# A hybrid decoder step in fp32 on one core: activations laid out with tokens along the columns from end to end, and the feed-forward of both pairs of blocks behind the fourth mixer

## The chip, the cores and the metric

The kernel runs on one core of a Trainium2 chip. The core's engines work side by side, each through its own list of instructions in order: PE (TensorE, matrix products into PSUM), DVE (VectorE), ACT (ScalarE), POOL (GpSimd) and SP (SyncE, which here only issues DMAs). ACT and POOL issue DMAs too. An instruction that needs a result of another engine waits for its semaphore, and everything behind it on the same engine waits with it. The metric is the device time of one execution in microseconds (us). Lower is better.

## The reference

2048 prompt tokens and 32 sample tokens (8 sequences of 4) of width 1024 go through one layer; everything is fp32.

```python
h = _rmsnorm(x, n1)
z = h @ w_in                       # hq hf hi hg | sq sk sv | ga gb
o_hg = hgrn2(hq, hf, hi)           # a gated recurrence over tokens, 4 heads
y_a = (_rmsnorm(o_hg, hg_norm_w) * silu(hg)) @ w_up_a
y_b = sliding_window_attention(sq, sk, sv) @ w_up_b
m = sigmoid(ga) * y_a + sigmoid(gb) * y_b
x = x + m @ w_o
h2 = _rmsnorm(x, n2)
x = x + square(relu(h2 @ w_ff1)) @ w_ff2      # 1024 -> 4096 -> 1024
y = _rmsnorm(x, normf_w)
```

`_rmsnorm` divides each token's row by the root of the mean of its 1024 squares and multiplies by a weight per column.

## The kernel before, in words

**Products.** Each fp32 product is made of three faster ones. Both operands are split into a high part (an ACT CAST to fp32r) and a low part (a DVE subtraction), and PE adds high x high, high x low and low x high. Every weight tile therefore passes a DMA on SP, a cast on ACT and a subtraction on DVE before PE can use it.

**Blocks and pairs.** The prompt is cut into four blocks of 512 tokens; the last also takes the 32 sample tokens. For each block a mixer runs on PE in this order: the input projections, attention, the recurrence, the gates, and last w_o (tile `wob`). Blocks 0 and 1 are pair 0, blocks 2 and 3 pair 1. The feed-forward runs on a whole pair, by one level of Strassen's scheme: FF1 (tiles `fB`, `fC`, `fD`) and FF2 (tile `f`; seven steps, whose results are added into `yacc`). The last step of FF2 is done in two column halves (`jp` = 0 and 1), each with four weight tiles of its own (`hw2T`, `lw2T`). Pair 1's operands have 528 columns per half and run in two chunks of 264; pair 0's have 512. Part of pair 1's input projection is done by Strassen's scheme too (stage z).

**Order of stages.** Block 0, block 1, FF1 and FF2 of pair 0, z, block 2, block 3, FF1 and FF2 of pair 1. Within a stage the code's order is the order on each engine, except where small generators and lists of pending steps (`late`, `todo`, `hook`) put pieces of one step between the products of another.

**Two layouts.** Products over tokens want the features on the partitions (here called transposed, as in `hT`). But x, the output of w_o and the two layer norms have the tokens on the partitions. A norm there is one ACT Square that sums along the row, two small POOL operations (L198, L200) and a scaling (`norm_pre`); then `norm_post` brings it into the transposed layout by 8 PE transposes of 128x128 for each 128 tokens (L225, tiles `tp_ab` for the first norm and `tp_fb` for the second), and DVE multiplies by the weight. w_o has the tokens as the stationary operand and 512 columns of w_o moving, so block 3 takes five token tiles, one of them with 32 rows. At the end of each FF2, `Fin` transposes `yacc` back (L1321, tile `fy`), adds the residual x (L1323), squares (L205), takes the root on POOL and scales (L1333), and stores. In FF2's last step PE does these transposes between its products. The norms of block 2 and 3 are done inside FF2 of pair 0 (tiles `x_n`), those of block 1 inside block 0's w_o (`x_b`).

## Time and profile before

| | |
|---|---|
| three runs | 2918.18, 2920.36, 2922.05 us; median 2920.36 |
| the profiled execution | 2911.64 us, of which the traced span is 2908.8 us; granted TensorE clock 0.991 on average |
| busy, of the span | PE 97%, DVE 59%, ACT 40%, POOL 16% |
| DMA | 471.78 MB, 162 GB/s on average |

A line of the trace has the start, the duration, the engine, the line of the kernel and the operation with its output and inputs; in brackets at its end stands how long the engine had been idle and what it waited for. Matrix products overlap in the array: a product with 512 moving columns is listed with 0.39 us, though the next one starts after less. So what a product costs PE is read from the distance of two starts, not from its listed duration. `x8` at the end of a row says that eight like instructions stand together in it.

### The profile page before, as it was taken

How to read it: one execution, taken by the hardware profiler on the slowest of the kernel's cores; microseconds unless marked ns; L12 is line 12 of the kernel's file. 1: busy time of each engine (PE TensorE's matmuls, PEld its weight loads, DVE VectorE, ACT ScalarE, POOL GpSimd, SP SyncE). 2: the span in 40 equal slices, each digit the busy share in tenths (PEclk: the TensorE clock that was granted, in tenths of full speed). 3: DMA queues.
4: the chain of work that ended last, by engine and by line, in shares of the span. 5: the costliest groups of instructions: out<-in, count | busy, mean ns of one | idle time of the engine just before them, and what ended most of it. 6: DMA issues, size and time to landing. Idle time of an engine off the chain costs nothing.

```text
span 2908.8 us, 50329 instructions
## 1 busy us (share of the span) xinstructions
PE 2814.7 (97%) x20207; PEld 2446.7 (84%) x20207; DVE 1705.9 (59%) x2739; ACT 1161.3 (40%) x2191; POOL 451.0 (16%) x791
## 2 busy tenths in 40 slices
PE   7999999999899999999999999999998999999997
PEld 6778887788788878887899867878888999999997
DVE  5684434734787764555765366446657777654455
ACT  3443334423433344543544433333334333344432
POOL 0110111101221110010310101120113333300001
PEclk9999999999999999999999999999999999999999
DMA  7756342145654475665743423423446444485552
GB/s 254 237 161 221 102 151 65 40 123 159 207 178 147 152 263 185 237 205 210 237 131 109 132 81 132 155 75 105 131 148 212 153 147 147 159 286 193 177 184 97
DMA packets 342354, 471.78 MB, mean 162 GB/s; under 512 B 27212, under 2 KB 216680, under 8 KB 342104
## 3 DMA queue, kind: packets, MB, share of 16 engines
q1 hardware_dynamic: 294096, 343.98, 37.2%
q0 software_dynamic: 33376, 105.76, 10.3%
q10 hardware_dynamic: 14648, 18.83, 1.8%
q8 instruction: 158, 2.59, 0.4%
q14 instruction: 76, 0.62, 0.1%
HBM read 345.15 MB, written 124.35 MB: 161 GB/s over the span
## 4 chain that ended last, share of the span: by engine, by line
PE 41%; DMA 3%; DVE 2%; issue 2%; POOL 1%; ACT 1%; SPq 0%; POOLq 0%; DVEq 0%; ACTq 0%
PE f L1349 3%; PE f L1350 3%; PE f L1351 3%; PE fB_f L238 2%; PE fB_f L240 2%; PE fB_f L239 2%; PE fB_z L238 1%; PE fB_z L240 1%; PE fB_z L239 1%; PE fD_f L240 1%; PE fD_f L238 1%; PE fD_f L239 1%; PE wob L191 1%; PE wob L193 1%; PE wob L192 1%
## 5 line engine op out<-in xcount | busy, mean ns | idle before, releaser
L1349 PE MATMUL f<-f2S,hw2T 128*128 128x264 f32 (+1 forms) x576 | 184.1, 320 | 0.0
L1351 PE MATMUL f<-f2S,lw2T 128*128 128x264 f32 (+1 forms) x576 | 183.5, 319 | 0.0
L1350 PE MATMUL f<-f2S,hw2T 128*128 128x264 f32 (+1 forms) x576 | 183.5, 319 | 0.0
L155 DVE TENSOR_TENSOR lw2T<-lw2T,hw2T 128x1024 fp32r<-128x1024 f32 x64 | 78.2, 1224 | 118.0 <-ACT hw2T L154 117.4
L238 PE MATMUL fB_f<-S,w1T_f 128*128 128x264 f32 (+1 forms) x384 | 123.0, 321 | 3.1 <-ACT c_f L300 2.6
L1349 PE MATMUL f<-f2A,h_w2B 128*128 128x264 f32 (+1 forms) x384 | 122.7, 320 | 0.6 <-ACT c_f L1242 0.6
L239 PE MATMUL fB_f<-S,w1T_f 128*128 128x264 f32 (+1 forms) x384 | 122.3, 319 | 0.0
L1350 PE MATMUL f<-f2A,h_w2B 128*128 128x264 f32 (+1 forms) x384 | 122.3, 319 | 0.0
L1351 PE MATMUL f<-f2A,l_w2B 128*128 128x264 f32 (+1 forms) x384 | 122.3, 319 | 0.0
L240 PE MATMUL fB_f<-S,w1T_f 128*128 128x264 f32 (+1 forms) x384 | 122.2, 319 | 0.0
L154 ACT CAST hw2T<-lw2T 128x1024 fp32r<-128x1024 f32 x64 | 67.3, 1051 | 131.8 <-DMA lw2T<-w_T 127.4
L1349 PEld LDWEIGHTS f<-f2S,hw2T 128*128 128x128 f32 x576 | 108.4, 188 | 7.6 <-DVE hw_ab L416 0.3
L1350 PEld LDWEIGHTS f<-f2S,hw2T 128*128 128x128 f32 x576 | 108.4, 188 | 7.3
L1351 PEld LDWEIGHTS f<-f2S,lw2T 128*128 128x128 f32 x576 | 108.0, 188 | 7.6
L155 DVE TENSOR_TENSOR f2S<-f2S 128x1024 fp32r<-128x1024 f32 (+1 forms) x64 | 79.0, 1240 | 56.1 <-ACT f2S L154 55.6
L230 ACT CAST w1T_f<-w1r_f 128x512 fp32r<-128x512 f32 x128 | 77.2, 619 | 69.2 <-PE fB_f L240 28.9
L231 DVE TENSOR_TENSOR l_w2B<-rw2B,h_w2B 128x1024 fp32r<-128x1024 f32 x48 | 58.8, 1224 | 76.8 <-ACT h_w2B L230 59.1
L231 DVE TENSOR_TENSOR w1T_f<-w1r_f,w1T_f 128x512 fp32r<-128x512 f32 x128 | 87.4, 688 | 23.6 <-ACT w1T_f L230 23.4
L1254 POOL DMA_DIRECT2D u_S<-s_f x144 | 77.7, 541 | 114.0 <-DVE s_f L1249 95.9
L1254 POOL DMA_DIRECT2D u_A<-c_f x104 | 56.2, 540 | 235.3 <-DVE c_f L1238 229.7
L154 ACT CAST f2S<-f2S 128x1024 fp32r<-128x1024 f32 (+1 forms) x64 | 67.9, 1064 | 53.5 <-DMA f2S<-u_S 51.1
L300 ACT COPY c_f<-fB_f 128x264 f32<-128x264 f32 (+1 forms) x80 | 36.1, 451 | 126.4 <-PE fB_f L240 117.3
(857 smaller groups left out, 9505.9 us busy)
## 6 DMA issues: line engine op xcount, KB each, us to landing
w1r_f<-w_ff SPq DMA_DIRECT2D x64, 512.0 KB
lw2T<-w_T SPq DMA_DIRECT2D x64, 512.0 KB
rw2B<-w_ff SPq DMA_DIRECT2D x48, 512.0 KB
f2S<-u_S SPq DMA_DIRECT2D x32, 528.0 KB
ws<-w_ff SPq DMA_DIRECT2D x64, 256.0 KB
r_wob<-w_o SPq DMA_DIRECT2D x32, 512.0 KB
f2S<-u_S SPq DMA_DIRECT2D x32, 512.0 KB
u_S<-s_f POOLq DMA_DIRECT2D x96, 132.0 KB, 2.3
```

The lines of the kernel that those rows point to most:

```text
L154: nc.scalar.copy(hi, F(lo))
L155: nc.vector.tensor_tensor(lo, F(lo), F(hi), ALU.subtract)
L230: nc.scalar.copy(dh, src)
L231: nc.vector.tensor_tensor(dl, src, F(dh), ALU.subtract)
L238: nc.tensor.matmul(ps, wh, ah, start=(first and k == 0), stop=False, skip_group_check=not first)
L239: nc.tensor.matmul(ps, wh, al, start=False, stop=False, skip_group_check=not first)
L240: nc.tensor.matmul(ps, wl, ah, start=False, stop=(last and k == 3), skip_group_check=not first)
L300: nc.scalar.copy(x, u.pB)
L1254: nc.gpsimd.dma_start(us[o][u.n // 4][u.n % 4 * P:(u.n % 4 + 1) * P, u.t0:u.t0 + u.ln], y_)
L1349: nc.tensor.matmul(ps, wh, ah, start=first, stop=False, skip_group_check=cont)
L1350: nc.tensor.matmul(ps, wh, al, start=False, stop=False, skip_group_check=cont)
L1351: nc.tensor.matmul(ps, wl, ah, start=False, stop=lastk, skip_group_check=cont)
```

## The change

The host lays x out transposed (`xT`, features by tokens, the sample tokens ahead of block 3), takes the output transposed (`yT`), and sends all norm weights as columns (`c_cols`). Then all of the kernel stays in the transposed layout:

- **Norms.** The sum over features is now a sum over partitions and over 8 row tiles. `Norm.add` squares one row tile on ACT into `na` or `nq` and POOL adds it on. `rstd_row` then multiplies the sum's columns by a column of ones on PE (one product with one moving column for every 128, 88 or 68 tokens; tile `n`), DVE adds the epsilon, POOL takes the root, PE spreads the result over all partitions by a transpose (tile `rb`), ACT copies it to SBUF, and DVE scales the eight row tiles. The 416 transposes of L225 and L1321 are gone; 88 one-column products and 60 transposes `rb` are new.
- **w_o** runs with its own columns as the stationary operand and the tokens moving: 192 products of 512 columns for a block, in block 3 192 of 288 and 192 of 256.
- **Order of stages:** block 0, block 1, z, block 2, block 3, then FF1 and FF2 of pair 0, then FF1 and FF2 of pair 1. The operand sums of the feed-forward are formed from `h2` in DRAM (`ff_sums`), for pair 0 during block 3's w_o, for pair 1 during FF2 of pair 0, and read back by POOL's DMAs.
- **The end of FF2.** `Fin` has one object for each half of the tokens. For each of 8 row tiles it loads x1 (the residual) into a buffer of the ring that also holds weights (`fx`, through `wtile`), adds, squares (`nq`, in the same ring) and sums; then comes `rstd_row`, and 8 scalings with 8 stores.

```diff
-    def norm_post(hsrc, nr, wcol, name, out):
-        for half in range(2):
-            tp = tp_ps(f"tp_{name}_{half}")
-            for kk in range(4):
-                k = half * 4 + kk
-                nc.tensor.transpose(tp[:, kk * P:kk * P + nr], hsrc[0:nr, k * P:(k + 1) * P], ident[0:nr, 0:nr])
...
+    def rstd_row(dst, sqs, n, tmp, name):
+        w = {256: 128, 512: 128, 264: 88, 528: 88, 544: 68}[n]
+        nt = n // w
+        ps = tp_ps(f"n_{name}")[0:w, 0:nt]
+        for i in range(nt):
+            for j, sq in enumerate(sqs):
+                nc.tensor.matmul(ps[:, i:i + 1], sq[:, i * w:(i + 1) * w], ones, start=(j == 0), stop=(j == len(sqs) - 1))
+        rs = tmp("ns", f"rs_{name}")[0:w, 0:nt]
+        nc.vector.tensor_scalar(rs, ps, EPS, None, ALU.add)
+        nc.gpsimd.tensor_tensor(rs, rs, negh[0:w].broadcast_to([w, nt]), ALU.pow)
+        for t0, ln in chunks_of(n):
+            rb = tp_ps(f"rb_{name}_{t0}")[:, 0:ln]
+            for i in range(ln // w):
+                c = t0 // w + i
+                nc.tensor.transpose(rb[:, i * w:(i + 1) * w], rs[:, c:c + 1].broadcast_to([w, P]), ident[0:w, 0:w])
+            nc.scalar.copy(dst[:, t0:t0 + ln], rb)
...
+        def add(u, x):
+            if u.acc is None:
+                u.acc = u.tmp("na", f"na_{u.N}")[:, 0:u.n]
+                nc.scalar.activation(u.acc, x, AF.Square)
+            else:
+                q = u.tmp("nq", f"nq_{u.N}")[:, 0:u.n]
+                nc.scalar.activation(q, x, AF.Square)
+                nc.gpsimd.tensor_tensor(u.acc, u.acc, q, ALU.add)
...
+        n2 = Norm(wk_tmp, T, n2c, f"f{B}")
+        for n in range(0, KD, 2):
+            uo = [unit_rows(w_o, 4 * kh, 4, n * P, 2 * P, f"wo{B}{n}{kh}") for kh in range(2)]
+            for j in range(n, n + 2):
+                js = slice((j - n) * P, (j - n + 1) * P)
+                for (t0, ln) in segs:
+                    ps = (sw_ps, mm_ps)[j % 2](f"wo{B}{j}_{t0}")
+                    gemm_T(ps, ln, [(uo[k // 4][0][:, k % 4, js], uo[k // 4][1][:, k % 4, js]) for k in range(KD)], m_acts, t0)
+                    xo = x1[:, j, t0:t0 + ln]
+                    nc.vector.scalar_tensor_tensor(xo, ps[:, 0:ln], 0.5, xo, ALU.mult, ALU.add)
+                n2.add(x1[:, j])
+                nc.gpsimd.dma_start(x1d[sb][j * P:(j + 1) * P, z0:z0 + T], x1[:, j])
...
+                def add(f, j):
+                    x = wtile(F32, f"fx_{f.N}{j}")[:, 0:f.ln]
+                    c0 = f.o * Th + f.t0
+                    nc.sync.dma_start(x, x1d[sb][j * P:(j + 1) * P, c0:c0 + f.ln])
+                    tt(f.y(j), f.y(j), x, ALU.add)
+                    f.n.add(f.y(j))
...
+                def out(f, j):
+                    f.n.scale(j, f.y(j))
+                    c0 = off[sb] + f.o * Th + f.t0
+                    (nc.sync if last else nc.gpsimd).dma_start(yT[j * P:(j + 1) * P, c0:c0 + f.ln], f.y(j))
...
+            todo = [lambda j=j: f0.add(j) for j in range(KD)] + [f0.end] + [lambda j=j: f0.out(j) for j in range(KD)]
+            todo += [lambda j=j, f=f: f.add(j) for f in f1 for j in range(4, KD)]
...
                         for g in range(KG):
                             for k in range(4):
...
-                            if not last:
-                                if f0 and g == 2 and (jp or j):
-                                    whole(f0.pop(0))
...
+                            for _ in range(2):
+                                if todo:
+                                    todo.pop(0)()
+                        evac(6, 2 * jp + j, f.t0, f.ln, ps)
+                        f.add(2 * jp + j)
```

Three places show how the order on the engines moves. The first is ACT at the boundary of the two column halves in the last step of pair 0's FF2. Before, the casts of the second half's weights (`hw2T_00_1` and on) stand among the squares of the output norm (`jkf`):

```order
L154 CAST hw2T_03_0_11034<-lw2T_03_0_11035 128x1024
L154 CAST f2A_0_11012<-f2A_0_11012 128x1024 x2
L205 ACTIVATE jkf_10989,fs_0_11127<-nj_10987 128x512 x2
L154 CAST hw2T_00_1_11163<-lw2T_00_1_11164 128x1024
L205 ACTIVATE jkf_10989,fs_128_11221<-nj_10987 128x512 x2
L154 CAST hw2T_01_1_11168<-lw2T_01_1_11169 128x1024
L154 CAST hw2T_02_1_11173<-lw2T_02_1_11174 128x1024
L154 CAST hw2T_03_1_11178<-lw2T_03_1_11179 128x1024
```

With the change, two squares of the first token half's sum (`nq`), the copy of its spread root (`na<-rb`) and two squares of the second token half stand right ahead of the first cast:

```order
L230 ACTIVATE nq_y_19288<-y_0_17440 128x512
L230 ACTIVATE nq_y_19294<-y_0_17441 128x512
L216 COPY na_y_19217<-rb_y_0_19324 128x512
L227 ACTIVATE na_y_19301<-y_0_17442 128x512
L230 ACTIVATE nq_y_19384<-y_0_17443 128x512
L147 CAST hw2T_00_1_19387<-lw2T_00_1_19388 128x1024
L147 CAST hw2T_01_1_19392<-lw2T_01_1_19393 128x1024
L147 CAST hw2T_02_1_19397<-lw2T_02_1_19398 128x1024
```

The first cast of the second half moved behind the whole output norm of the first token half.

The second place is DVE at the same boundary (`y_0_17434` to `17441` are the first token half's eight row tiles, `y_0_17443` is the second one of the other token half, `fx` is the residual, `cols` holds the norm weight). Before, no row of DVE there depends on more than 128 tokens at a time. Now:

```order
L209 TENSOR_SCALAR rs_y_19321<-n_y_19316 128x4
L1284 TENSOR_TENSOR y_0_17442<-y_0_17442,fx_y_19298 128x512
L237 SCALAR_TENSOR_TENSOR y_0_17434<-y_0_17434,cols,na_y_19217 128x512
L237 SCALAR_TENSOR_TENSOR y_0_17435<-y_0_17435,cols,na_y_19217 128x512
L237 SCALAR_TENSOR_TENSOR y_0_17436<-y_0_17436,cols,na_y_19217 128x512
L237 SCALAR_TENSOR_TENSOR y_0_17437<-y_0_17437,cols,na_y_19217 128x512
L237 SCALAR_TENSOR_TENSOR y_0_17438<-y_0_17438,cols,na_y_19217 128x512
L237 SCALAR_TENSOR_TENSOR y_0_17439<-y_0_17439,cols,na_y_19217 128x512
L237 SCALAR_TENSOR_TENSOR y_0_17440<-y_0_17440,cols,na_y_19217 128x512
L1284 TENSOR_TENSOR y_0_17443<-y_0_17443,fx_y_19381 128x512
L237 SCALAR_TENSOR_TENSOR y_0_17441<-y_0_17441,cols,na_y_19217 128x512
L148 TENSOR_TENSOR lw2T_00_1_19388<-lw2T_00_1_19388,hw2T_00_1_19387 128x1024
```

Seven scalings of whole row tiles moved ahead of the addition to `y_0_17443`, whose square is the last row of ACT ahead of the cast above.

The third place is SP in the last step of pair 1's FF2, the end of the program. Before, the weights of the second column half (`lw2T_10_1` to `lw2T_13_1`) stand at its start or between stores:

```order
L1305 DMA f2A_1_26977<-u_A_2_1_19863 128x2x528 x2
L1289 DMA lw2T_13_0_27007<-w_T_236 128x4x256
L1289 DMA lw2T_10_1_27332<-w_T_236 128x4x256
L1305 DMA f2A_1_26984<-u_A_3_1_19864 128x2x528 x2
L1289 DMA lw2T_11_1_27337<-w_T_236 128x4x256
L1334 DMA out_y_sample<-nj_26959 16x512 x2
L1334 DMA out_y_prompt<-fx_1_26960 128x512 x6
L1289 DMA lw2T_12_1_27342<-w_T_236 128x4x256
L1334 DMA out_y_prompt<-fx_1_26960 128x512 x2
L1289 DMA lw2T_13_1_27347<-w_T_236 128x4x256
L1334 DMA out_y_sample<-nj_26959 16x512 x2
L1334 DMA out_y_prompt<-fx_1_26961 128x512 x8
```

With the change, a store of the first token half's last row tile and nine loads of the residual stand ahead of them:

```order
L1293 DMA out_yT<-y_1_23862 128x528
L1283 DMA fx_y_26984<-x1d_96 128x264
L1283 DMA fx_y_26990<-x1d_96 128x264
L1283 DMA fx_y_27008<-x1d_96 128x264
L1283 DMA fx_y_27014<-x1d_96 128x264
L1283 DMA fx_y_27031<-x1d_96 128x264
L1283 DMA fx_y_27037<-x1d_96 128x264
L1283 DMA fx_y_27044<-x1d_96 128x264
L1283 DMA fx_y_27063<-x1d_96 128x264
L1283 DMA fx_y_27106<-x1d_96 128x264
L1250 DMA lw2T_10_1_27113<-w_T_218 128x4x256
L1250 DMA lw2T_11_1_27118<-w_T_218 128x4x256
```

The weights of the second half moved behind eight stores (one is shown) and behind the loads `fx` of the second token half; what the first of these loads needs is the scaling of the last row tile that is stored ahead of it.

More of the change, by code (lines that the diff above doesn't have):

```diff
@@ L734, in tile_hybrid_step @@
             while late:
-                norm_post(*late.pop(0))
+                late.pop(0)()
             for h in range(HH):
@@ new lines, in tile_hybrid_step @@
+                            for _ in range(2):
+                                if todo:
+                                    todo.pop(0)()
+                        evac(6, 2 * jp + j, f.t0, f.ln, ps)
+                        f.add(2 * jp + j)
+                    if jp == 1:
+                        while todo:
+                            todo.pop(0)()
+                        f.end()
+                        for j in range(KD):
+                            f.out(j)
+_INS = ["cache_swa_k", "cache_swa_v", "state_hgrn", "w_in", "sinks", "w_up_a", "w_up_b", "w_o", "w_ff1", "w_ff2"]
```

595 lines of the change are left out of this document (236 added, 359 removed).

## The prediction

> **What bounds the kernel now.** I read the page's busy shares and slices first, then PE's rows around the stage boundaries, then the groups of lines for prices.
>
> ```profile
> span 2908.8 us, 50329 instructions
> PE 2814.7 (97%) x20207; PEld 2446.7 (84%) x20207; DVE 1705.9 (59%) x2739; ACT 1161.3 (40%) x2191; POOL 451.0 (16%) x791
> PE   7999999999899999999999999999998999999997
> PEclk9999999999999999999999999999999999999999
> ```
>
> PE is busy in every slice but the first and last, at full clock; the others have slack on average. So a change pays by what it takes off PE, and costs whatever makes PE wait. What a product costs is the distance of two starts. These rows are PE in the last step of FF2 of pair 0, at the boundary of the column halves:
>
> ```profile
> 1364.02 0.39 PE L1349 MATMUL f<-f2A,hw2T 128*128 128x512 f32 x1
> ...
> 1365.16 0.40 PE L1351 MATMUL f<-f2A,lw2T 128*128 128x512 f32 x1
> 1365.39 1.04 PE L1321 MATMUL fy<-ident,yacc 128*128 128x128 f32 x8
> 1366.19 0.48 PE L1349 MATMUL f<-f2A,hw2T 128*128 128x512 f32 x1
> ...
> 1368.52 0.55 PE L1321 MATMUL fy<-ident,yacc 128*128 128x128 f32 x3 [1.16 <-DVE nj L1323]
> 1369.65 0.50 PE L1351 MATMUL f<-f2A,lw2T 128*128 128x512 f32 x1 [0.58 <-DVE lw2T L155]
> ```
>
> Five products of 512 columns from 1364.02 to 1365.16: 0.228 each. Eight transposes from 1365.39 to 1366.19: 0.10 each, though listed at 0.27. And at this boundary PE waited only 1.16 + 0.58 = 1.74 us. Two more distances, from FF2 of pair 1:
>
> ```profile
> 2874.85 0.29 PE L1349 MATMUL f<-f2A,hw2T 128*128 128x272 f32 x1
> ...
> 2875.98 0.29 PE L1349 MATMUL f<-f2A,hw2T 128*128 128x272 f32 x1
> 2892.77 0.28 PE L1351 MATMUL f<-f2A,lw2T 128*128 128x256 f32 x1
> ...
> 2893.13 0.28 PE L1351 MATMUL f<-f2A,lw2T 128*128 128x256 f32 x1
> ```
>
> 272 columns: 1.13 / 9 = 0.126. 256 columns: 0.36 / 3 = 0.12. In proportion 288 cost 0.133.
>
> **The change, part by part.** The sum is made against the profiled execution, 2911.64, and the difference is put on the median of the runs, 2920.36, which lies 8.7 us above it.
>
> (a) The transposes removed: 416.
>
> ```profile
> L225 PE MATMUL tp_fb<-ident,y_b x64: 270/272/328, 407.5 to 1907.1; 128*128 128x128 f32 x64
> L225 PE MATMUL tp_fb<-ident,h_b x64: 270/273/424, 738.3 to 2211.8; 128*128 128x128 f32 x64
> L225 PE MATMUL tp_ab<-ident,x_n x64: 270/272/273, 1138.3 to 1320.8; 128*128 128x128 f32 x64
> L225 PE MATMUL tp_ab<-ident,x_first x32: 271/347/476, 10.6 to 23.9; 128*128 128x128 f32 x32
> L1321 PE MATMUL fy<-ident,yacc x144: 270/272/329, 1361.8 to 2894.7; 128*128 128x128 f32 x128, 128*16 128x128 f32 x16
> ```
>
> The 32 of `x_first` belong to the start (e). 384 x 0.10 = -38. All lie in PE's order, so all count while PE is the bound. The Trainium skill ("TensorE: Matmul & The Clock Gate", Part 4) gives about 275 ns for a transpose in a kernel's context; by that the term would be 384 x 0.275 = -106. The listed 272 agrees with the page, but the distance of starts does not, so the sum doesn't use it.
>
> (b) w_o of block 3: 5 token tiles x 48 = 240 products of 512 columns become 192 of 288 and 192 of 256: 192 x 0.253 - 240 x 0.228 = -6. The other blocks keep 192 of 512. The last step of pair 1's FF2 is cut 264 + 264 instead of 272 + 256: nothing.
>
> (c) New on PE: 56 one-column products and 56 spreading transposes (32 and 4 more at the start). The trace has no one-column product; the nearest row is the transpose, 0.10. As an fp32 product may be two passes, a product costs 0.10 to 0.20: 5.6 to 11, the transposes 5.6. I take +12.
>
> For the waits these prices are needed:
>
> ```profile
> L1073 POOL TENSOR_TENSOR ta_b<-ta_b,pb_b 128x512 f32<-128x512 f32 x14 | 18.1, 1296 | 216.4 <-DVE ta_b L1048 216.4
> L1073 POOL TENSOR_TENSOR ga_b<-ga_b,pb_b 128x256 f32<-128x256 f32 x7 | 5.2, 741 | 4.1 <-DVE ga_b L1048 4.1
> L200 POOL TENSOR_TENSOR ors_b2o<-ors_b2o,negh 128x4 f32<-128x4 f32 x4 | 4.1, 1018 | 0.3
> L1360 DVE TENSOR_TENSOR yacc<-f,yacc 128x512 f32<-128x512 f32 x24 | 15.6, 683 | 2.5 <-PE f L1351 2.4
> L1360 DVE TENSOR_TENSOR yacc<-f,yacc 128x264 f32<-128x264 f32 x40 | 14.5, 424 | 9.6 <-PE f L1351 8.6 <-ACT yacc L1358 0.9
> L1333 DVE SCALAR_TENSOR_TENSOR nj<-nj,fr,nfb 128x512 f32<-128x512 f32 x16 | 11.4, 749 | 9.4 <-POOL fr L200 9.4
> L205 ACT ACTIVATE nj<-fx 128x512 f32<-128x512 f32 x16 | 10.1, 632 | 23.8 <-DVE fx L1323 21.6 <-DVE yacc L1360 2.0
> L1358 ACT COPY yacc<-f 128x512 f32<-128x512 f32 x16 | 9.2, 580 | 3.0 <-PE f L1351 3.0
> L154 ACT CAST hw2T<-lw2T 128x1024 fp32r<-128x1024 f32 x64 | 67.3, 1051 | 131.8 <-DMA lw2T<-w_T 127.4 <-PE f L1350 4.2
> u_S<-s_f POOLq DMA_DIRECT2D x96, 132.0 KB, 2.3
> 2865.34 4.14 DMA lw2T<-w_T
> ```
>
> (d) Each norm puts the chain one-column products, DVE, POOL root (1.02), spread into PE's own order, with 2 to 13 products behind the first to cover it (0.5 to 3 us against some 1.9). At six places away from stage boundaries about 1 us each: +5 (2 to 15, as POOL's additions of 1.3 can also be late; in block 1's w_o it has 21 of them, 27 us, beside its DMA issues, in 45 us).
>
> (e) The start: 32 transposes and the loading of norm rows by PE go; eight squares, the chain and eight scalings (8 x 0.75) on DVE ahead of the last row tile come. 0 (-6 to +6).
>
> (f) Stage boundaries.
>
> ```profile
> 745.00:800.00 55.00, 46.82 (x201) 37.70 (x200) 43.28 (x66) 25.22 (x39) 16.55 (x24) 0.94 0.76 240
> 1345.00:1450.00 105.00, 97.51 (x535) 83.19 (x533) 67.91 (x97) 43.73 (x84) 26.11 (x56) 0.98 0.63 211
> 2170.00:2240.00 70.00, 60.61 (x346) 51.97 (x345) 49.51 (x90) 31.69 (x54) 25.51 (x39) 0.90 0.69 214
> 755.00:760.00 5.00, 1.48 (x8) 0.90 (x6) 2.03 (x4) 1.22 (x2) 3.57 (x6) 1.00 1.07 366
> 760.00:765.00 5.00, 5.00 (x19) 4.35 (x20) 4.53 (x7) 4.00 (x6) 1.73 (x3) 0.66 0.99 353
> ```
>
> Columns: window, length, PE busy, PEld, DVE, ACT, POOL, granted clock, DMA share, GB/s. The three stretches are block 1 to FF1, FF2 to z, block 3 to FF1. Idle time plus what the clock took (length x (1 - clock)): 8.2 + 3.3, 7.5 + 2.1 less the 1.7 of the half boundary, 9.4 + 7.0: 36 us. After an idle of 3.5 us the clock stands at 0.66 for 5 us: a long wait costs 1.7 us more. After the change: block 1 to z some 6 (operand sums on DVE behind two projections), block 3 to FF1 some 5 (pair 0's operands are ready), and FF2 of pair 0 to FF1 of pair 1. There the last output norm ends in PE's order ahead of the first `fB`: evacuation, addition, square, POOL addition, root, spread with four ACT casts and four DVE subtractions of other operands between them, some 12 us; then eight scalings (6 us) stand on DVE ahead of the low half of the first w1 tile, of which 4 us bite. With 1 for the switch itself 28 in all. I take -10 (-25 to +2).
>
> (g) The half boundary of pair 0. By the order shown above, from PE's last product on: evacuation 0.45 + 0.69, two additions 1.37, square 0.63, POOL addition 1.3, one-column products, root and spread 2.5, copy 0.58, seven scalings 5.25, addition 0.68, square 0.63, cast 1.05, with semaphores some 16 us until PE has weights. Less the rows of (c) in it and the 1.74 lost now: +13. Nothing covers it: on PE the next row is a product of the second half.
>
> (h) The half boundary of pair 1. The same up to the copy (9 us, in 528 columns), then eight scalings to 15, the last store, then the load `fx` behind it on SP, 2.3 (132 KB); addition, square and POOL additions (0.42, 0.4, three of 0.74) to 20.5; only then SP issues the first weight load, as its buffer held one of the squares: 4.14, cast 1.05: PE stands some 25 us, and the first pass then runs at the pace of the loads. Less 2 lost there now: +23.
>
> (i) The tail after the last product: evacuation to root about as now, then eight scalings of 264 columns (8 x 0.43) against two of 0.75: +2.
>
> (j) The clock after the two new waits, 2 x 1.7 = +3.
>
> Sum: -38 - 6 + 12 + 5 + 0 - 10 + 13 + 23 + 2 + 3 = +4. So 2915.6 for a profiled execution and 2924 for the median: +0.13%, where about 0.2% (5.8 us) is what a measurement can tell from no change. PE has 32 us less to do for norms and w_o, and stands still 36 us longer.
>
> **The rivals.**
> - *Cover (faster).* If the first half's norm is finished before PE gets to the boundary, and the weights are loaded by then, (g), (h), (j) and half of (f)'s last term fall: 13 + 23 + 3 + 8 = 47 less, 2877; with only pair 1's wait gone, about 2899. For it: today the same place costs 1.74 us, with the same additions, squares and scalings. Against it: the rows of ACT, DVE and SP in the part on the change, where whole row tiles stand ahead of the first cast.
> - *Reloads one by one (slower).* In (h) I let the nine loads `fx` overlap. They share a ring with the squares and the weights. If each waits for the buffer that the one before frees (2.3 + 0.42 + 0.4 = 3.1 us), the last five behind the first store take 15 us more than I gave them: 2939. It decides from about +2 us for (h). For it: SP issues in order, and `fx` is loaded under the same tag as the weights. Against: the ring turns over many buffers there.
> - *The transposes stood in waits (slower).* If the 240 transposes of L225 only filled time in which PE would have waited for the next stage, (a) shrinks to 144 x 0.10 = -14: 2948. Against: their tiles spread over the whole run, and only those of `h_b` end at boundaries.
> - *A transpose costs PE its listed time (faster).* If a transpose held PE for the 0.272 us that its rows list, (a) would be 384 x 0.272 = -104 instead of -38: 2858. The eight starts at 0.10 speak against it. This is what the Trainium skill's figure, named in (a), would make of it.
>
> **How the numbers follow.** The sum's own case has 0.54, from 2910 to 2938 by the bounds of (c), (d), (f): of it 0.11 below 2914.5, 0.20 within 0.2%, 0.23 above. Cover has 0.23, reloads 0.13, stood in waits 0.08, listed time 0.02. Faster: 0.23 + 0.02 + 0.11 = 0.36. Same: 0.20. Slower: 0.13 + 0.08 + 0.23 = 0.44. The range leaves out the far half of Cover and the listed time below, and Stood in waits above: 2882 to 2945.
>
> **What would show it.** In the trace after: no L225 or L1321 rows, and `n` and `rb` rows at starts 0.1 apart (a, c); `wob` of block 3 at 0.133 and 0.12 (b); one idle of some 14 to 16 us ahead of the first `f` of the second half in FF2 of pair 0, released by ACT `hw2T`, with seven scalings on DVE just before (g); one of 20 to 27 us at the same place of pair 1, released by the load of `lw2T`, with `fx` loads ahead of it on SP (h); FF2 to FF1 with PE idle some 16 us in two pieces (f). The prediction is wrong if these waits are a few us, or if new idle time of more than 15 us stands at the start, in block 1's w_o behind POOL's additions, or at the opening of z or FF1, none of which the trace of before can show.

## The result, and the profile after

The changed kernel takes 2985.71 us (median of four runs, 2984.10 to 2986.99) against 2919.27 for the kernel before (2916.92 to 2922.05): ratio 1.0227, 95% interval 1.0209 to 1.0245. It is 2.3% slower, and the prediction of 2924 (2882 to 2945) is missed by 62 us.

The head of the page after:

```profile
span 2982.3 us, 50304 instructions
PE 2823.5 (95%) x20169; PEld 2461.4 (83%) x20169; DVE 1720.7 (58%) x2742; ACT 1131.4 (38%) x2128; POOL 556.0 (19%) x825
PE   8999999999899999999998999999987999999995
PEclk9999999999899999999999999999988999999997
```

PE's share fell from 97 to 95%, with holes at slices 11 (block 1's w_o), 22 (the end of block 3's w_o and the opening of FF1) and 30 and 31 (the end of FF2 of pair 0). Its busy time grew from 2814.7 to 2823.5 us, where the prediction gave it 32 us less to do, and its idle time (the span less the busy time) grew by 65 us, from 94 to 159, where the prediction had 36. Four of the entries of what PE waited for, from the view of waits (total us, times, longest):

```profile
PE f L1297 <- ACT hw2T L147: 28.4, 3, 18.5
PE n_y L207 <- POOL na_y L231: 26.8, 4, 14.9
PE n_z L207 <- POOL na_z L231: 8.4, 2, 4.7
PE n_h L207 <- POOL na_h L231: 6.2, 1, 6.2
```

The largest entry of this list before was 7.2 us in total. To place the loss, the span is cut at the first product of each stage on PE (FF2 at the first one behind the last product of FF1, since a few `f` products stand ahead of it). The last column is the best version that the experiments led to (e18, below). The profiled execution of the kernel before is one of its fastest, so the sum of the differences is 7 us more than the difference of the medians.

| stretch on PE | before | after | difference | e18 less before |
|---|---|---|---|---|
| start to `ps_hqb` of block 0 | 43.1 | 53.7 | +10.6 | +5.5 |
| rest of block 0's mixer | 295.0 | 289.8 | -5.2 | -6.1 |
| w_o of block 0 | 47.6 | 54.2 | +6.6 | +1.4 |
| block 1's mixer | 320.0 | 321.1 | +1.1 | -1.7 |
| w_o of block 1 | 46.2 | 62.8 | +16.6 | +11.2 |
| small projections and z | 250.3 | 245.2 | -5.1 | -9.8 |
| block 2's mixer | 186.2 | 181.0 | -5.2 | +5.3 |
| w_o of block 2 to block 3's `ps_hib` | 89.9 | 96.3 | +6.4 | +7.9 |
| block 3's mixer from there | 224.1 | 229.0 | +4.9 | +5.2 |
| w_o of block 3 | 59.0 | 59.3 | +0.3 | -1.6 |
| FF1 of pair 0 | 322.3 | 320.6 | -1.7 | +2.3 |
| FF2 of pair 0, to the next stage | 318.8 | 351.6 | +32.8 | +8.5 |
| FF1 of pair 1 | 354.8 | 347.7 | -7.1 | +1.3 |
| FF2 of pair 1, to the end | 351.5 | 370.0 | +18.5 | -2.0 |
| sum | 2908.8 | 2982.3 | +73.5 | +27.4 |

Each kernel has one profile, and a stage that an edit left alone is not always equally long: over the experiments most such stages vary by 2 to 7 us, and block 3's mixer by 12 (224.4 in e10, 236.3 in e14). A difference of that size in one row of one run shows nothing yet.

**The half boundaries.** PE's rows at the boundary of pair 0 after, with DVE's row of the scalings among them:

```profile
2200.48 0.39 PE L1299 MATMUL f<-f2A,lw2T 128*128 128x512 f32 x1
2205.72 1.86 PE L207 MATMUL n_y<-ones,na_y 128*128 128x1 f32 x8 [4.85 <-POOL na_y L231]
2209.35 1.11 PE L215 MATMUL rb_y<-ident,rs_y 128*128 128x128 f32 x4 [1.77 <-POOL rs_y L210]
2211.18 4.73 DVE L237 SCALAR_TENSOR_TENSOR y<-y,cols,na_y 128x512 f32<-128x512 f32 x7 [2.79 <-ACT na_y L216]
2218.16 0.80 PE L1297 MATMUL f<-f2A,hw2T 128*128 128x512 f32 x1 [7.69 <-ACT hw2T L147]
```

From the last product of the first half to the first of the second 17.7 us pass on PE. What stands in them is the chain of step (g): addition, norm, seven scalings, and only then the weights' cast. And at pair 1's boundary, whose last product started at 2914.07:

```profile
2919.04 1.92 PE L207 MATMUL n_y<-ones,na_y 128*88 128x1 f32 x12 [4.69 <-POOL na_y L231]
2922.79 1.14 PE L215 MATMUL rb_y<-ident,rs_y 88*128 88x88 f32 x6 [1.82 <-POOL rs_y L210]
2942.47 0.59 PE L1297 MATMUL f<-f2A,hw2T 128*128 128x264 f32 x1 [18.55 <-ACT hw2T L147]
```

Here 28.4 us pass. SP issued the first load of the second half's weights at 2937.57, behind nine loads `fx`.

**FF2 of pair 0 to FF1 of pair 1.** The last `f` product started at 2242.78. PE's rows, four rows of DVE, and two windows (columns as in the prediction):

```profile
2258.08 1.87 PE L207 MATMUL n_y<-ones,na_y 128*128 128x1 f32 x8 [14.92 <-POOL na_y L231]
2262.28 1.12 PE L215 MATMUL rb_y<-ident,rs_y 128*128 128x128 f32 x4 [2.33 <-POOL rs_y L210]
2264.64 0.59 PE L248 MATMUL fB_f<-A,w1B_f 128*128 128x264 f32 x1 [1.25 <-ACT w1B_f L240]
2270.15 0.39 PE L250 MATMUL fB_f<-A,w1B_f 128*128 128x264 f32 x1 [2.50 <-DVE w1B_f L241]
2249.21 0.68 DVE L1284 TENSOR_TENSOR y<-y,fx_y 128x512 f32<-128x512 f32 x1
2249.81 1.25 DVE L148 TENSOR_TENSOR S<-S 128x1056 fp32r<-128x1056 f32 x1
2253.43 1.26 DVE L148 TENSOR_TENSOR A<-A 128x1056 fp32r<-128x1056 f32 x1 [2.37 <-ACT A L147]
2254.60 0.68 DVE L1284 TENSOR_TENSOR y<-y,fx_y 128x512 f32<-128x512 f32 x1
2245.00:2250.00 5.00, 0.00 (x0) 0.00 (x0) 3.83 (x5) 2.74 (x5) 3.84 (x4) 0.77 0.99 297
2250.00:2255.00 5.00, 0.00 (x0) 0.00 (x0) 2.63 (x3) 2.14 (x3) 2.08 (x2) 0.50 1.04 377
```

PE has nothing for 15 us ahead of the one-column products of the last norm; meanwhile the DMA engines are full with pair 1's operands (`S`, `A`) and w1, and the splits of these operands, which wait for their loads, stand on DVE and ACT between the additions (L1284) and squares that this norm is made of.

**w_o.** The windows of w_o of blocks 0 and 1, after (first two) and before:

```profile
340.00:400.00 60.00, 53.80 (x232) 44.40 (x231) 30.45 (x37) 23.93 (x36) 26.80 (x23) 0.91 0.44 145
715.00:785.00 70.00, 59.77 (x268) 48.65 (x267) 28.66 (x37) 27.34 (x44) 37.99 (x37) 0.90 0.58 191
336.00:387.00 51.00, 50.68 (x240) 42.03 (x240) 27.31 (x36) 19.37 (x27) 2.63 (x6) 1.00 0.38 124
704.00:753.00 49.00, 49.00 (x230) 40.78 (x229) 29.20 (x40) 20.08 (x26) 8.89 (x13) 1.00 0.68 210
```

Before, PE was full at full clock; after, it idles for 6 and 10 us and the mean clock is 0.91 and 0.90, while POOL's work grew from 2.6 to 26.8 and from 8.9 to 38.0 us.

**The start.**

```profile
11.26 11.34 PE L207 MATMUL n_first<-ones,sq 128*128 128x1 f32 x52 [1.50 <-ACT sq L431]
24.05 1.11 PE L215 MATMUL rb_first<-ident,rs_first 128*128 128x128 f32 x4 [1.45 <-POOL rs_first L210]
27.28 0.80 PE L184 MATMUL ps_hib<-h_hib,hT 128*128 128x512 f32 x1 [2.11 <-ACT hT L240]
27.87 0.63 PE L185 MATMUL ps_hib<-l_hib,hT 128*128 128x512 f32 x1
28.30 0.63 PE L184 MATMUL ps_hib<-h_hib,hT 128*128 128x512 f32 x1
```

Each fp32 one-column product is two records, so the 32 products of the start are 64. 52 of them take 11.34: 0.218 each. The first projection begins at 27.3; before it began at 18.1.

### The profile page after: what moved, and what is told of

Read it like the earlier page. It is cut to its first block, busy times and chain, and to the rows that moved or that the text cites. A ratio compares the mean times of both kernels' runs of the same rounds, so it can differ in the third digit from the quotient of the medians.

```text
span 2982.3 us, 50304 instructions
## 1 busy us (share of the span) xinstructions
PE 2823.5 (95%) x20169; PEld 2461.4 (83%) x20169; DVE 1720.7 (58%) x2742; ACT 1131.4 (38%) x2128; POOL 556.0 (19%) x825
## 4 chain that ended last, share of the span: by engine, by line
PE 76%; DMA 6%; issue 6%; POOL 5%; DVE 4%; ACT 2%; POOLq 0%; SPq 0%; ACTq 0%; DVEq 0%
PE f L1297 6%; PE f L1299 6%; PE f L1298 6%; PE fB_f L248 4%; PE fB_f L250 3%; PE fB_f L249 3%; PE fD_f L250 2%; PE fD_f L248 2%; PE fD_f L249 2%; PE fB_z L248 1%; PE fB_z L250 1%; PE fB_z L249 1%; PE ps_hgb L161 1%; PE ps_hgb L162 1%; PE ps_hgb L163 1%
## 5 line engine op out<-in xcount | busy, mean ns | idle before, releaser
L231 POOL TENSOR_TENSOR na_y<-na_y,nq_y 128x512 f32<-128x512 f32 (+2 forms) x35 | 39.2, 1120 | 554.7 <-ACT nq_y L230 553.7
L161 PE MATMUL wob<-m_b,h_wob 128*128 128x512 f32 (+2 forms) x320 | 115.9, 362 | 12.0 <-DVE x_b L1158 5.3
L162 PE MATMUL wob<-m_b,h_wob 128*128 128x512 f32 (+2 forms) x320 | 116.0, 362 | 1.1 <-DVE m_b L241 1.1
L163 PE MATMUL wob<-m_b,l_wob 128*128 128x512 f32 (+2 forms) x320 | 115.6, 362 | 0.0
L241 DVE TENSOR_TENSOR l_w2B<-rw2B,h_w2B 128x1024 fp32r<-128x1024 f32 x48 | 58.7, 1223 | 75.5 <-ACT h_w2B L240 61.6
```

The lines of the kernel that those rows point to most:

```text
L161: nc.tensor.matmul(ps[:, 0:n], wh, rh, start=(k == 0), stop=False)
L162: nc.tensor.matmul(ps[:, 0:n], wh, rl, start=False, stop=False)
L163: nc.tensor.matmul(ps[:, 0:n], wl, rh, start=False, stop=(k == nk - 1))
L241: nc.vector.tensor_tensor(dl, src, F(dh), ALU.subtract)
```

## The experiments

All times below are medians. Each ratio is to the kernel before, timed again beside the run, and stands with its 95% interval. Where only stage times decide, they are cut at PE's rows as in the table.

**e1: the output stage's buffers out of the weight ring.** Theory "ring": in (g) and (h) the weights wait for buffers that `fx` and `nq` hold in the ring.

```diff
-                    x = wtile(F32, f"fx_{f.N}{j}")[:, 0:f.ln]
+                    x = fxb[f.o][:, j, f.t0:f.t0 + f.ln]
...
-                    f.n.add(f.y(j))
+                    f.n.add(f.y(j), x)
...
+            fxb = [raw8(6, Th, f"fx0_{sb}"), raw8(0 if last else 6, Th, f"fx1_{sb}")]
```

> The changed kernel, but in the last step of FF2 the loaded residual (fx) and its square (nq) get a buffer of their own (operand slot 6, for the last half slot 0) instead of the ring that holds the weights. The changed kernel took 2985.7. Theory 'ring': at the column-half boundaries PE stands 17.7 us (pair 0) and some 27 us (pair 1) because the squares and reloads of the output norm take ring buffers ahead of the second half's weights; with buffers of their own both waits fall to about 3 us, as before the change: 2985.7 - 15 - 24 = about 2947 (2940 to 2958). Rival 'chain': the norm's own chain in the order of ACT and DVE (squares, root, scalings ahead of the cast) holds the weights whatever the buffers are; then only the late load of pair 1 goes: 2976 or more.

2952.05 us, ratio 1.0130 (1.0105 to 1.0155): by the medians 34 us of the loss are gone, by the ratios some 28. The waits on `hw2T` are gone, others remain (the two rows of ACT stand at pair 0's boundary):

```profile
PE n_y L207 <- POOL na_y L231: 16.1, 5, 5.9
PE fB_f L248 <- ACT c_f L310: 11.1, 9, 3.0
PE fC_f L248 <- DVE p_f L325: 5.9, 1, 5.9
2196.10 1.05 PE L207 MATMUL n_y<-ones,na_y 128*128 128x1 f32 x8 [3.58 <-POOL na_y L231]
2201.14 1.12 PE L215 MATMUL rb_y<-ident,rs_y 128*128 128x128 f32 x4 [3.42 <-POOL rs_y L210]
2186.76 1.04 ACT L147 CAST hw2T<-lw2T 128x1024 fp32r<-128x1024 f32 x1
2202.35 0.59 ACT L216 COPY na_y<-rb_y 128x512 f32<-128x512 f32 x1 [1.79 <-PE rb_y L215]
2890.49 1.85 PE L207 MATMUL n_y<-ones,na_y 128*88 128x1 f32 x12 [3.75 <-POOL na_y L231]
2240.00:2250.00 10.00, 4.08 (x24) 3.86 (x22) 4.74 (x4) 5.57 (x7) 2.37 (x2) 0.67 0.74 245
```

FF2 of pair 1 to the end takes 350.5, a little less than before the change, so pair 1's 28 us came with the ring. At pair 0's boundary the order on ACT moved with the buffers: two casts of the second half's weights, at 2180.93 and 2186.76, now stand ahead of the copy of the first half's root (2202.35), where in the changed kernel all four followed it (from 2217.08 on). So e1 shows that the ring held the weights; it does not separate the wait for a buffer from the order that came of it. FF2 of pair 0 takes 321.2 (after: 351.6), but FF1 of pair 1 takes 364.1 (after: 347.7): 16 us come back as waits inside FF1's opening. The window shows PE with 4.08 us of work in 10 there. That the total lies in the range of theory "ring" is in part luck: the two FF2 stages gained 50 us where it expected 39, and FF1 gave back 16 that it did not expect.

**e15 and e9: what comes back in FF1.** e15 gives pair 0 two small buffers and leaves operand slot 6 to FF1; e9 is e1 with pair 0's last step cut into two pieces, as pair 1's is.

```diff
 # e15, against e1
-            fxb = [raw8(6, Th, f"fx0_{sb}"), raw8(0 if last else 6, Th, f"fx1_{sb}")]
+            fxb = [raw8(6 if o == 0 else 0, Th, f"fx{o}_{sb}") for o in range(2)] if last else None
...
+                    ... else fp.tile([P, Th], F32, tag="fx", bufs=2, name=f"fx_{f.N}{j}")
 # e9, against e1
-            cut = Th // 2 if last else Th
-            f1 = [Fin(1, t0, ln) for t0, ln in (((0, cut), (cut, Th - cut)) if last else ((0, Th),))]
+            cut = Th // 2
+            f1 = [Fin(1, t0, ln) for t0, ln in ((0, cut), (cut, Th - cut))]
```

> As e1_own, but for pair 0 the residual and its square use two small buffers beside the accumulators instead of operand slot 6; pair 1 as in e1_own. e1_own took 2952.1: FF2 of both pairs became about as short as before the change, but FF1 of pair 1 got 16 us longer than in the changed kernel (364 against 348). Theory 'slot': that is since slot 6 now comes free only with the last addition, and S2, the operand of pair 1 that is loaded there, comes late; with slot 6 left alone FF1 of pair 1 falls back by 10 to 16 us, and FF2 of pair 0 stays within 4: 2937 to 2944. Rival 'norm in front': FF1 of pair 1 is late because the output norm of pair 0's second token half, now beside it instead of ahead of it, has the engines first: within 4 us of 2952.

> As e1_own, but pair 0's last step is cut into two token quarters of 256 as pair 1's is into 264 + 264, so that half of the second output norm is done a quarter earlier. 192 products of 512 become 384 of 256: 384 x 0.12 - 192 x 0.228 = +2.3. Theory 'norm in front' (the second output norm stands in front of FF1 of pair 1): half of its eight scalings and squares go ahead, 5 to 9 less in FF1: 2945 to 2950. Rival 'slot' (late operands): 2954, the 2.3 us more alone.

e15: 2956.39 us, ratio 1.0142 (1.0118 to 1.0165); FF2 of pair 0 and FF1 of pair 1 together 690.9, in e1 685.3. FF1 of pair 1 alone takes 366.6, so it isn't the slot. (The total is 4.3 above e1, just outside the 4 that "norm in front" allowed, with overlapping intervals.) e9: 2949.35 us, ratio 1.0119 (1.0090 to 1.0148); the same two stages 678.6 (before 673.6), FF1 alone 352.1. Less norm work in front of FF1 shortens it, as "norm in front" says; the totals of e9 and e1 overlap, so this rests on the stage times of one profile each.

**e3 and e14: POOL's additions in w_o.** e3 lets DVE add the squares, e14 gives the squares a second buffer and leaves the additions on POOL.

```diff
 # e3, in Norm.add (the output norms stay on POOL)
-                nc.gpsimd.tensor_tensor(u.acc, u.acc, q, ALU.add)
+                u.eng.tensor_tensor(u.acc, u.acc, q, ALU.add)
 # e14
-        ... bufs=(na_bufs if tag == "na" else 1), name=name) ...
+        ... bufs=(na_bufs if tag == "na" else 2), name=name) ...
```

> The changed kernel, but the squares of the norms inside w_o (not of the output norm) are added on by DVE instead of POOL. Theory 'POOL': in w_o of blocks 0, 1 and 2 PE waits in its own order for a sum of squares that POOL builds at 2.07 us a row tile (1.3 for the addition, 0.65 for the square that waits for it, with one buffer between them); DVE adds in 0.69, a row tile then takes some 1.4, and the waits of 6.2, 4.7 and 3.6 us mostly go, with the half-clock stretch behind each: 10 to 18 less, 2968 to 2976. Rival 'one buffer and loads': ACT's squares and the loads of x set the pace, or DVE, which also evacuates w_o, becomes late itself: within 4 us of 2985.7, or above.

> The changed kernel (2985.7) with two buffers instead of one for the squares of the norms inside w_o of blocks 1 and 3 (block 0 and 2 have a ring of three already); POOL still adds. In e3_dve, where DVE adds, the sum of w_o fell by about 10 us, 9.6 in all: 8 in block 0's, 9 in block 1's, with 3 given back in block 2's. Theory 'one buffer': in block 1's w_o square and addition alternate, 2.07 us a row tile; with two buffers 1.4, and the two waits of 4.7 and 3.6 us there go: 5 to 9 less, 2977 to 2981. Rival 'POOL': its queue (additions, stores) is what is late: at most 3 less.

e3: 2976.12 us, ratio 1.0216 (1.0185 to 1.0248), by its median some 10 less than the changed kernel; but one of its four runs took 2991, and its interval overlaps that of the changed kernel (1.0209 to 1.0245), so the total alone shows no gain, and what follows rests on stage times. e14: 2986.55 us, ratio 1.0237 (1.0215 to 1.0258), no change, although its additions follow each other at 1.37 us (four in 5.46) where they had been 2.07 apart. PE's wait for `n_z` did not fall (10.4 us, in the changed kernel 8.4), so it isn't the one buffer. The one-column products of block 0's w_o, after (first two rows) and in e3:

```profile
371.15 1.87 PE L207 MATMUL n_h<-ones,na_h 128*128 128x1 f32 x8 [6.20 <-POOL na_h L231]
372.88 0.77 PE L162 MATMUL wob<-m_b,h_wob 128*128 128x512 f32 x1
366.77 1.02 PE L207 MATMUL n_h<-ones,na_h 128*128 128x1 f32 x8 [0.70 <-DVE na_h L231]
367.65 0.49 PE L162 MATMUL wob<-m_b,h_wob 128*128 128x512 f32 x1
```

With the wait, the same eight records take 1.73 us (0.216 each); without it 0.88 (0.11). The wait costs its own 6.2 us, doubles the price of what follows, and the next products of 512 columns too run at 0.43 instead of 0.23. In e3 block 0's w_o fell from 54.2 to 46.0 and block 1's from 62.8 to 53.8. These gains are clear of the scatter: the seven kernels in which POOL adds there (the changed one, e1, e4, e9, e10, e14, e15) take 53.5 to 55.1 and 61.6 to 64.2. In the w_o of blocks 2 and 3 e3 gained nothing (96.0 and 60.9, after 96.3 and 59.3). And from block 1's w_o to block 2's first product e3 takes 308.0 us, like the changed kernel (308.0). What it gained in block 1's w_o it lost in the stage behind.

**e4 and e10: the start.** e4 has DVE add the eight squares, so that 4 products replace 32; e10 is e4 without seven of the eight scalings.

```diff
+    for k in range(1, KD):
+        tt(sq0[:, 0], sq0[:, 0], sq0[:, k], ALU.add)
-    rstd_row(rb0, [sq0[:, k] for k in range(KD)], bt, wk_tmp, "first")
+    rstd_row(rb0, [sq0[:, 0]], bt, wk_tmp, "first")
```

> The changed kernel, but at the start DVE adds the eight squared row tiles of the first block (7 additions of 0.69 us), and PE multiplies one sum instead of eight: 4 one-column products instead of 32. Theory 'price': a one-column product takes PE two passes of 0.21 us, so the 32 stand for 11.3 us in a row behind the last square; 4 take 1.7, the last addition 0.7: 9 less, 2977. Rival 'load': the first product of the input projection waits for the loads of x and weights and for DVE's eight scalings anyway: at most 3 less, 2983 or more.

> As e4_start, but of the eight row tiles of the first block only the first is scaled; the scaling of the other seven is left out. In e4_start PE's first projection ended (start of the next one) at 50.3 us, against 53.7 in the changed kernel and 43.1 before. Theory 'DVE': scalings (0.69) and low parts (0.63) of the eight row tiles stand on DVE and ACT ahead of the weights' casts and low parts, which PE waits for: without seven scalings the next projection starts 4 to 6 us earlier, at 44 to 46. Rival 'weights': the weights' loads set it: within 1 us of 50.3.

e4: 2984.02 us, ratio 1.0228 (1.0207 to 1.0249). Its first projection begins at 22.2 (after: 27.3), and `ps_hqb` at 50.3 (53.7). e10 (one run, 2980.47): 23.0 and 47.6, between the two figures named: from the first projection to `ps_hqb` 24.6 us, in e4 28.1, before 25.0. So of the 10.6 us that the start had grown, 3.4 went with the products, 2.7 with DVE's scalings ahead of the weights' low parts, and 4.5 remain: the first projection still begins 4 to 5 us later. These shares are rough, for the kernels that keep the changed start take 53.7 to 56.6 to `ps_hqb` (the changed one, e1, e3, e9, e14, e15, e19) and those with e4's start 48.6 to 50.3 (e4, e16, e17, e18); by them the products were worth 3 to 8 us, and e10's 2.7 is little more than the scatter. In the total e4 gained nothing: block 2's mixer took 190.4 instead of 181.0 us with the same order of instructions in it. Rows and windows at its beginning, in e4:

```profile
1035.37 1.11 PE L769 MATMUL qT_b2c<-ident,qkv_b 128*128 128x128 f32 x4 [4.10 <-POOL qkv_b L766]
1030.00:1035.00 5.00, 1.27 (x6) 0.70 (x4) 1.23 (x1) 1.37 (x2) 3.18 (x5) 0.83 0.98 346
1035.00:1040.00 5.00, 4.63 (x25) 3.80 (x25) 0.00 (x0) 1.70 (x3) 4.39 (x11) 0.50 0.02 6
```

PE waits 4.1 us for data that came late from full DMA engines (`qkv_b`), then runs at half clock.

**e5: the one-column products twice**, to price them in place.

```diff
-            for j, sq in enumerate(sqs):
+            for j, sq in enumerate(sqs + sqs):
...
```

> The changed kernel, but every one-column product is issued twice (176 instead of 88; the second set overwrites the first). Theory 'price': each product costs PE 0.43 us (128 tokens), 0.29 (88) or 0.12 (68) wherever it stands, since nothing covers it: 13.6 at the start and 18 elsewhere more, 3017. By the prediction's price of 0.10 to 0.20 it would be 10 to 18 more, 2996 to 3004. Rival 'hidden': outside the start the products stand in waits that have another end: 13 more at most, 2999 or less.

3027.90 us, ratio 1.0383 (1.0365 to 1.0400): 42 us for 88 products more, 0.48 each, over the price forecast. 16 of the 42 lie at the start (`ps_hqb` at 69.8 instead of 53.7), where the added 64 records stand back to back with the others:

```profile
11.31 25.04 PE L207 MATMUL n_first<-ones,sq 128*128 128x1 f32 x116 [1.34 <-ACT sq L431]
15.00:20.00 5.00, 5.00 (x26) 5.00 (x25) 0.00 (x0) 0.00 (x0) 0.00 (x0) 1.00 0.64 258
```

25 us pass without a gap, all at 0.216 a record, and the clock column says 1.00 (more on this at the end).

**e16 to e19: put together.** e16 is e9 with e4's start and with the squares of the input norms (`h`, `z`) added by DVE, those of the feed-forward norm by POOL. e17 ends a norm one step later; e18 also scales z's second half behind the small projections; e19 is e18 with the changed kernel's start.

```diff
 # e17
-lambda: [nn.add(xr[:, k]) for k in range(4, 8)] + [nn.end()]]
+lambda: [nn.add(xr[:, k]) for k in range(4, 8)], lambda: nn.end()]
...
-            todo = [lambda j=j: f0.add(j) for j in range(KD)] + [f0.end] + ...
+            todo = [lambda j=j: f0.add(j) for j in range(KD)] + todo[:2] + [f0.end] + ...
 # e18
+            late += zt[1][4:]
```

> All four mendings in one kernel: the output stage's buffers of e1 and pair 0's last step in two pieces (e9), the start's squares summed by VectorE into one product a piece (e4), and the squares of the input norms (h and z) in the output projections of blocks 0 and 1 added by VectorE, while GpSimd keeps those of the feed-forward norm. Theory 'sum' (the parts lie in different stages and add): 2949 of e9, less 3 for the start (e4), less 17 for the projections of blocks 0 and 1 (e3 gained 8.2 and 9.0 there and lost 4.8 in blocks 2 and 3, whose additions stay on GpSimd here): 2929, between 2925 and 2934, 0.4 to 0.6% above before. Rival 'displaced' (what VectorE adds is late for the evacuations, or the feed-forward norm's additions on GpSimd were the slow ones): 2938 or more.

> e16, and the end of a norm (its one-column products and the spreading) comes one step of the projection, or two additions of the output stage, after the norm's last addition, so that TensorE has products to do while the sum is finished. Theory 'in order' (the waits on n_h, n_z and pair 0's n_y, 6.2, 8.4 and 4.8 us in the changed kernel and more in slow products behind them, come from the place of these products in TensorE's order): 8 to 15 us less than e16, 2914 to 2921, within 0.2% of before. Rival 'chain' (the norm, scaling and split are the longer chain, so a later end only moves the wait to the operands of the next projection): within 4 us of e16.

> e17, and the second half of pair 1's input is scaled and stored behind the small projections that follow block 1's output projection (they read the first half alone), so that VectorE makes the low parts of their weights first. Theory 'chain' (in e16 TensorE had 2.95 us of work between 760 and 770 while VectorE scaled that half until 768.2, ahead of l_skvb: what the shorter projection gained was given back there): from block 1's output projection to block 2's first product 307.1 us of e17 fall to 297 to 301 (before: 296.5), and the time to 2928 to 2933. Rival 'loads' (the small projections or pair 1's sums then wait for loads or for the stored half): that stretch stays within 3 us of 307, and the time within 4 of e17.

> e18 with the start as in the changed kernel (32 products, no sum on VectorE). In e4, e10, e16 and e17, which begin their projections 3 to 4 us earlier, block 2 from its first product to its output projection took 187 to 191 us, against 177 to 178 in the changed kernel and e9, with the instructions of block 2 in the same order: in e4 TensorE waited 4.1 us for qkv_b at block 2's begin and ran at half clock after it. Theory 'phase' (the shift by a few us decides whether block 2's first loads are late): without the start's sum block 2 takes 177 again or, if e18's other shifts have moved it, anything up to 188; start 3.5 longer, total between 5 less and 3 more than e18. Rival 'start' (the sum itself is worth 3 us and block 2 has another cause): block 2 as in e18, total 3 to 4 us more than e18.

| | us | ratio to before, 95% | w_o of block 1 | from it to block 2's first product |
|---|---|---|---|---|
| e16 | 2943.13 | 1.0088 (1.0071 to 1.0105) | 49.5 | 305.1 |
| e17 | 2938.20 | 1.0077 (1.0060 to 1.0095) | 59.7 | 303.4 |
| e18 | 2934.82 | 1.0055 (1.0036 to 1.0073) | 57.4 | 297.9 |
| e19 | 2941.53 | 1.0080 (1.0061 to 1.0099) | 58.4 | 300.8 |

e16 missed its sum by 14 us, as its rival "displaced" said, though not where that rival looked. w_o of block 1 is even shorter than forecast, but the stretch to block 2 is only 2.9 shorter than in the changed kernel, and block 2's mixer takes 190.1. DVE and a window in e16, behind that w_o:

```profile
762.27 6.01 DVE L237 SCALAR_TENSOR_TENSOR zh<-zh,cols,na_z 128x528 f32<-128x528 f32 x8 [3.22 <-ACT na_z L216]
768.20 1.21 DVE L241 TENSOR_TENSOR l_skvb<-r_skvb,h_skvb 128x1024 fp32r<-128x1024 f32 x1
760.00:770.00 10.00, 2.95 (x21) 2.52 (x21) 7.73 (x10) 2.53 (x5) 8.13 (x12) 0.82 0.57 211
```

The eight scalings of z's second half stand on DVE ahead of the low part that PE needs next. e17 moved the wait more than it removed it (4.9 us less than e16, with overlapping intervals), so "chain" describes it better. e18 took the scalings out of the way: the stretch fell by 5.5 us against e17 (by its first product; the 307.1 of the expectation counts to the second group of products, where e18 has 301.6, just outside the 297 to 301 of "chain"). The total fell by 3.4 to 2934.8, above the 2928 to 2933 of "chain" and within the 4 us of its rival, with overlapping intervals; so the stretch speaks for "chain", and the total for neither. e19: block 2 is back at 183.2 us and the start 6.5 longer; the total, 6.7 more, fits neither forecast. No version beats the kernel before.

## Why the prediction was wrong, point by point

- **(a), the transposes removed, was right**: by count times median distance of starts, products of 128 columns cost 39 us less in all, against 38 (the 39 counts the start's transposes and the new ones `rb` too). Whether some of them had stood in waits no run separates.
- **(b)** is right in price (0.133 and 0.12 from start to start) and invisible in time: block 3's w_o takes 59.3 against 59.0. Before, PE worked through all of it; after, it works 52.0 us and idles 7.3. Its longest wait there, 5.0 us, is for an evacuation on DVE (`x_b`), which stands behind a low part of w_o's weights that itself waited 3.3 us for its cast.
- **(c) was too low, 12 against some 24** (distances of starts, idle time left out), and its rule fell short in one thing. A warm product costs 2 x 0.112 = 0.22, just over the bound of 0.20. But products that follow a wait cost 2 x 0.213. The Trainium skill ("TensorE: Matmul & The Clock Gate", Part 2, on LDWEIGHTS) gives columns / 1.2 ns for loading a stationary operand, by estimate 107 ns for 128; by that and two passes a product would be 0.21, again an estimate. The warm records agree. The prediction also says that the trace of before has no one-column product, and that is wrong: the recurrence has 256 of them, two records each, on stationary operands of 32 columns. They showed the two passes, but not the price of a wide one, for 64 records take 0.64 us, from 190.56 to the next product at 191.20:

```profile
190.56 0.71 PE L647 MATMUL lx_b0g<-W_b 128*32 128x1 f32 x64 [0.56 <-DVE W_b L619]
```

- **(d), the norms in w_o, is the step that failed most**: +5 (2 to 15), where the four w_o stretches grew by 30 us in spite of (b), and PE's idle time in them from 0.3 to 28.4. I counted only the short chain from products to root, and gave POOL's additions a share in the range instead of a place in PE's order. In w_o of blocks 0 and 1, which grew by 23 us, the wait is for these additions: with them on DVE (e3) 17 of the 23 go, and e16 keeps them away. The rows show that a wait of 6 us costs half clock after it too, and e16 that shortening it uncovers DVE's scalings behind. The other 7 us, in blocks 2 and 3, did not go with the additions; there PE waits for casts (`m_b`) and for `x_b`, and no run tested why.
- **(e), the start: 0 (-6 to +6) against +10.6.** 32 products at 0.43 replaced transposes that had overlapped the arriving rows. e4 and e10 divide it, roughly: 3.4 for the products, 2.7 for DVE's scalings ahead of the low parts, and 4.5 that are left, in which the first projection begins later; that this is the norm's chain is argued, not shown.
- **(f), FF2 to FF1: 16 forecast, some 24 measured**: from the last `f` product to the first `fB` 21.9 us pass, and PE waits 2.5 more at the first low half. The chain was the one described; the splits of arriving operands stand between its steps longer than forecast. The two other switches came out as forecast: 6 and 5 us, where PE's idle time and the clock take 6.9 behind block 1 (782 to 840) and 5.3 behind block 3 (1592 to 1640). The term itself was added up wrongly: by its own figures it is 28 - 36 = -8, not -10.
- **(g) and (h) were right**: 17.7 against 16, 28.4 against 25, and PE goes on when the weights (`hw2T`) come, behind the rows that the prediction named. The idle time comes in three pieces around the norm's products, not in one. But e1 shows that this chain need not have held the weights: they waited for ring buffers, which (h) names for one load and (g) not at all. With buffers of its own, FF2 of pair 1 costs no more than before.
- **(i)** had the wrong sign, -3 instead of +2: the last product starts 12.5 us before the end, where it was 15.7 before (2893.13 of 2908.8):

```profile
2969.76 0.28 PE L1299 MATMUL f<-f2A,lw2T 128*128 128x264 f32 x1
2972.43 0.63 PE L207 MATMUL n_y<-ones,na_y 128*88 128x1 f32 x6 [2.39 <-POOL na_y L231]
```

- **(j)**, 3 for the clock behind the two boundaries, came out at about 4.5: the products start at the half rate until 2223.7 and 2947.3. The slow clock behind the waits in w_o had no term.

So the two half boundaries, which I worked out row by row in the order, came out within 4 us each, and the switch from FF2 to FF1 within 8. The places that I priced with "about 1 us each" or "0" hold most of the miss. Of the rivals none is it: (h) came out 3 us over its term, far from the 15 of the reloads one by one (SP issued the nine loads within 5.9 us), and no rival spoke of w_o and the start, which the prediction only named as places that the trace of before could not show. There it asked for more than 15 us of new idle time in one place; block 1's w_o has 10, and the miss is a sum of several smaller ones.

What stays open is, first, why block 2's mixer takes 190 to 191 us in the four measured kernels e4, e16, e17 and e18 (and in e10), which sum at the start, and 181 to 188 in all others, with its own instructions in the same order. The rows of e4 show late loads and the clock; no run tells why the start decides it. The last 27 us of e18 lie in the table: most of them in w_o of block 1, FF2 of pair 0 and w_o of block 2 (for the +7.9 of the last no cause was tested); block 3's mixer (+5.2) is within its scatter.

## What to carry to other kernels

A layout that saves transposes moves a norm's sum from one accumulation along the row, within ACT's square, into a chain over four engines, and each end of that chain stands in the matrix engine's own order: put the price on the wait for the last addition, not on the few products, and count the slow clock after it. Buffers for results should not come from the ring that feeds the next weights: that was worth some 30 us here. When a wait is taken away, look at the next stage's first operand before counting the gain: 16 of the 50 us that e1 gained in FF2 stood in FF1 again, and 10 of the 13 that e16 gained in block 1's w_o stood in the stage behind.

## What was not expected of the hardware

- The price of a product with one moving column goes by the width of its stationary operand: 0.112 us a record for 128 columns, 0.078 for 88, 0.062 for 68, two records for each fp32 product, and about twice that after a wait (0.213 and 0.147 for 128 and 88).
- A stream of such products stays slow: 25 us of them back to back at 0.216 in e5. The clock column prints 1.00 in these windows only because the trace's record of the clock begins later: its first entry, full clock, stands at 45.3 us in e5 and at 32.4 in the changed kernel, which is where the products of 512 columns pass from 0.43 to 0.23 from start to start. So at the start read the rate from the starts. The Trainium skill ("TensorE: Matmul & The Clock Gate", Part 1) says that the warm-up is some 3.4 us of time, whatever is issued in it; the 25 us disagree for products of this kind. With products of 512 columns the full rate came after 3.4 us in e5 (41.88 to 45.3) and 5.1 in the changed kernel (27.28 to 32.4), nearer to the page.
